# Layer B's Strassen operand sums: by adding DMA from DRAM in place of vector operations on GpSimd

## The chip, the cores and the metric

The kernel runs on one core of a Trainium2 chip. The metric is the device time of one execution in microseconds (us); smaller is better. The program works on TensorE (PE: matmuls), VectorE (DVE), ScalarE (ACT), GpSimd (POOL) and the queues from which DMA transfers are issued (SyncE, SP; ScalarE and GpSimd issue some too).

## The reference

Two layers of a decoder trunk on 1024 tokens of width 1024, in float32. Layer A is a gated MLP, layer B a Mamba-2 (SSD) mixer; each adds its output to the residual, and a last RMSNorm follows. What concerns the change is layer B's input projection:

```
proj   = rmsnorm(h) @ w_in                    # 1024 x 1024  times  1024 x 6176
z      = proj[..., :2048]                     # gate, silu(z) multiplies the output
xbc    = silu(conv(proj[..., 2048:6144]))     # causal convolution of 4 taps along the tokens
dt     = softplus(proj[..., 6144:] + dt_bias) # 32 heads; decays exp(cumsum(dt * A)) come from it
```

## The kernel before, in words

**Products.** float32 matmuls are made of three in the fast format: an operand is split into a high part (a rounding cast on ScalarE, `split`, L111) and a low part (the difference, L112, on VectorE), and `mm3` (L134 to L136) adds high x high, low x high and high x low into one accumulator. In tile names `wh` and `wl` are a weight operand's two parts, `hh` and `hl` those of the activations.

**Blocks.** Most of layer B's input projection is done in eight `Block`s. A block multiplies the 1024 tokens by 512 columns of w_in (256 in the half block) as a 2 x 2 product with seven half-size products in place of eight (Strassen's scheme in Winograd's form). The weight quarters are b00, b01 (upper half of the rows, left and right columns) and b10, b11. Four sums of them are needed:

```
t1 = b01 - b00        (L204, operand of product 5)
t2 = b11 - t1         (L205, operand of product 6)
t7 = b11 - b01        (L214, over b01, operand of product 7)
t4 = b10 - t2         (L212, over b10, operand of product 4)
```

Products 1, 2 and 3 take b00, b10 and b11 as they are. `Block.prep(n)` makes an operand (with its sum, when it has one) and splits it; `Block.mm(n, i)` issues the matmuls of unit i; `Block.post` hands a finished quarter to the block's `done`; `Block.run` does all in the order 1, 2, 6, 7, 4, 5, 3. Each quarter is loaded by SyncE (`load_raw`, L120). The sums run on the block's engine `eng`.

**Which blocks, in order.** Block 0 to 3 give z (`z_block`, block 3 with 128 columns in place of 256 per half), and four blocks give x and B, C of the groups 0, 1 and then 3, 5 (`xbc_block`). They run as z block 0, 1, 2; x(0,1); bc(0,1); x(3,5); z block 3; bc(3,5). Sums are on GpSimd in block 0 (the fourth on VectorE), on VectorE in z blocks 1 and 2, and on GpSimd in all the rest; z block 3 also has its low parts made on GpSimd.

**Around them.** Block 0 is interleaved by hand with the end of layer A (`into_b`, a manual schedule): the residual rows are normalised (`norm`, L971), transposed on TensorE (L977), and GpSimd forms sums of activations (`s31`, L1014 and L1015) and the start of each row's 1/sqrt (`rsqrt_a`, tile `rr`, L141). Behind product 6 of z block 1 stand the `decays` (L1140 to L1189): a chain of small VectorE operations from `dtr` to dt (L1146 to L1158), scans, three pairs of transposes on TensorE (L1186), and SyncE's writes of `cs_d`, `ecs_d` and of `dec_d`, whose elements are single numbers. Everywhere but in `into_b` a scheduler orders the instructions of each engine by its own estimates; each engine then works through its list strictly in order, and an instruction that waits holds up all behind it.

**What leaves a block.** A z quarter goes through a tile `zt` (pool k2, three buffers; sum on VectorE L913, silu on ScalarE L915) and is written to DRAM by GpSimd's queue (`z_d`, L917). An xbc quarter is added on VectorE into `u` (L1240), and `convolve` works off the convolution's taps (VectorE, L1205, and L1208 for the few columns at the seam, `halo`), with ScalarE before and after. `u` also names the tile to which ScalarE copies a product (L252). Raw weights have four buffers (`wr`), high and low parts three each, accumulators six.

Of the kernel before, what the change touches and what calls it, by code (L numbers as in the profile page):

```python
# [11 lines left out]
ALU = mybir.AluOpType  # L12
# [3 lines left out]
P = 128  # L16
# [13 lines left out]
def kernel(  # L30
# [21 lines left out]
    nc = tc.nc  # L52
    x = x[0]
    out = out[0]
# [13 lines left out]
    def q4(shape, name):  # L68
        return sb.tile(shape, F32, name=name, tag="q4", bufs=6)
# [112 lines left out]
    class Block:  # L182
# [5 lines left out]
        def __init__(self, H, W, token_major, done, eng=nc.vector, cols=256):  # L188
            self.H, self.W, self.token_major, self.done, self.eng = H, W, token_major, done, eng
            self.cols, self.units = cols, 2 if token_major else cols // P  # L190
            self.b, self.Y, self.acc, self.u, self.wide, self.t2 = {}, {}, {}, {}, False, None

        def load(self, kh, j):
            self.b[kh, j] = load_raw(self.W(kh, j), 4)

        def sums(self):
            if self.t2 is None:
                b, TT = self.b, self.eng.tensor_tensor
                if self.wide:
                    t12 = s8([P, 2, 4, 256], "t12")  # L200
                    self.t1, self.t2 = t12[:, 0], t12[:, 1]
                else:
                    self.t1, self.t2 = q4([P, 4, self.cols], "t1"), q4([P, 4, self.cols], "t2")
                TT(out=self.t1, in0=b[0, 1], in1=b[0, 0], op=ALU.subtract)  # L204
                TT(out=self.t2, in0=b[1, 1], in1=self.t1, op=ALU.subtract)  # L205

        def prep(self, n, lo=None):
            b, TT = self.b, self.eng.tensor_tensor
            if n in (4, 6):
                self.sums()  # L210
            if n == 4:
                TT(out=b[1, 0], in0=b[1, 0], in1=self.t2, op=ALU.subtract)  # L212
            if n == 7:
                TT(out=b[0, 1], in0=b[1, 1], in1=b[0, 1], op=ALU.subtract)  # L214
            src = {1: b[0, 0], 2: b[1, 0], 4: b[1, 0], 7: b[0, 1], 3: b[1, 1]}.get(n)
            if src is None:
                src = self.t1 if n == 5 else self.t2
            h_, l_ = wh([P, 4, self.cols]), wl([P, 4, self.cols])
            split(h_, l_, src, lo)
            self.Y[n] = (h_, l_)  # L220

        def mm(self, n, i, post=True, halves=(0, 1)):
            Xh, Xl = self.H[("A11", "A12", "S4", "A22", "S1", "S2", "S3")[n - 1]]
# [340 lines left out]
    for g in range(G):  # L564
# [26 lines left out]
        def mix(m, th):  # L591
            c = g * 2 + m
            mx = sm("mx")
            for q in range(4):
# [11 lines left out]
        blk = Block(HS, lambda kh, j: [a_w_in[kh * 512:(kh + 1) * 512, j * DI + g * 256:j * DI + (g + 1) * 256]],  # L606
                    False, done_zu)
# [10 lines left out]
    class Out:  # L618
# [82 lines left out]
        def add(self, dst, src):  # L701
            nc.gpsimd.dma_start(out=dst, in_=src, accum_op=ALU.add)
# [154 lines left out]
    H2 = {}  # L857
# [47 lines left out]
    def z_block(b, eng=nc.vector):  # L905

        wide = 256 if b < 3 else 128

        def done(name, i, a, u):
            th, j = 2 - int(name[1]), int(name[2]) - 1  # L910
            zt = k2([P, 512], "zt")
            if u is not None:
                nc.vector.tensor_tensor(out=zt, in0=a, in1=u, op=ALU.add)  # L913
                a = zt
            nc.scalar.activation(zt, a, AF.Silu)  # L915
            g, m = (2 * b + j, i) if b < 3 else (6, j)
            nc.gpsimd.dma_start(out=z_d[g][:, m, th * 512:(th + 1) * 512], in_=zt)  # L917

        def W(kh, j):
            c = 512 * b + j * wide  # L920
            return [b_w_in[kh * 512:(kh + 1) * 512, c:c + wide]]

        return Block(H2, W, False, done, eng, wide)

    def dt_load():

# [30 lines left out]
    zb = [z_block(b) for b in range(4)]  # L957

    def into_b():


        V, S, Gp = nc.vector, nc.scalar, nc.gpsimd
        TTv, TTg = V.tensor_tensor, Gp.tensor_tensor
        blk = zb[0]
# [52 lines left out]
        def s2(tt):  # L1017
            f0 = F[1, tt][:, 0]
            TTv(out=f0, in0=F[0, tt][:, 1], in1=f0, op=ALU.subtract)
            hi("S2", tt, f0)  # L1020
            lo("S2", tt, f0)
# [49 lines left out]
        ao.post(3, 3), ao.rstd_a(0, 3), store_h1(0, 3, 1)  # L1071
        second(1)
        s31(1)
        blk.sums()
        norm(0, 3, rs(3))
        s2(0), both("S3", 0, S3[0])
        blk.prep(2)
# [2 lines left out]
        second(2)  # L1080
        s31(2)
        s2(1), both("S3", 1, S3[1])
        blk.mm(1, 0, False)
        tr(0, 3)
        second(3)
        s31(3)
        blk.eng = V
        blk.prep(4)
        blk.eng = Gp
        s2(2), s2(3)  # L1090
        blk.mm(1, 1, False)
        for i in range(2):
# [38 lines left out]
        for i in range(2):  # L1131
            blk.post(3, i), nxt.post(1, i)

    zb[0].eng, zb[0].wide = nc.gpsimd, True
    with tc.manual_schedule():
        into_b()
    tok_of = {}
    V = nc.vector
# [75 lines left out]
    def xbc_block(kind, gs):  # L1214

        held, halos = {}, {}

        def cols(j):
            if kind == "x":
                return [(DI + gs[j] * 256, 256)]  # L1220
            return [(2 * DI + j * 1024 + g * P, P) for g in gs]

        def W(kh, j):
            return [b_w_in[kh * 512:(kh + 1) * 512, c:c + n] for c, n in cols(j)]

        def out(th, i, j, src, halo=None):
            if kind == "x":
                g, m, c = gs[j], i, cols(j)[0][0] + i * P
            else:
                g, m, c = gs[i], 2 + j, cols(j)[i][0]  # L1230
            dst = k2([P, 512], "xc")
            for op in conv_ops(dst, src, (c - DI) // P, halo):
                op()
            nc.scalar.activation(dst, dst, AF.Silu)
            nc.scalar.dma_start(out=xbc_d[g][:, th, m, :], in_=dst)

        def done(name, i, a, u):
            th, j = 2 - int(name[1]), int(name[2]) - 1
            if u is not None:
                nc.vector.tensor_tensor(out=u, in0=a, in1=u, op=ALU.add)  # L1240
# [12 lines left out]
        b = Block(H2, W, False, done, nc.gpsimd)  # L1253
        b.wide = True
        return b

# [560 lines left out]
```

## Time and profile before

| | |
|---|---|
| median of 3 runs | 1625.0 us (1624.87 to 1628.37) |
| the profiled execution | 1622.94 us |
| its span, first to last instruction | 1621.2 us |
| mean granted TensorE clock | 0.969 |
| GpSimd busy | 466.8 us (29%) |
| VectorE busy | 1085.5 us (67%) |

The profile has one row per instruction with its start from the span's beginning, its duration, the engine, the line of the kernel, the tiles (output <- inputs, `x` and a number for equal instructions drawn together), and in brackets how long the engine had stood idle before it and what ended that. The waits view adds these idle times up by pair: who waited, for whom, total, times, longest. A DMA row gives the transfer's size and the median time from issue to landing. z block 0 begins at about 720 us and bc(3,5) ends at about 1070 us.

### The profile page before, as it was taken

The page shows a single profiled execution, that of the slowest core. Times are in us where ns is not written, and L with a number is a line of the kernel's source. Part 1 is how long each engine was busy: PE and PEld are TensorE (multiplying, and loading weights), DVE is VectorE, ACT ScalarE, POOL GpSimd, SP SyncE. Part 2 cuts the span into 40 slices and gives each one's busy share as a digit, 9 for nine tenths or more (in the row PEclk, how much of TensorE's full clock was granted, in tenths as well). Part 3 has the DMA queues.
Part 4 walks back from the last instruction along what each step waited for, and adds up shares of the span by engine and source line. Part 5 has one row for each costly group of instructions (what it writes and reads, how often), then busy time and mean ns, then how long its engine had stood idle before and what let it go on. Part 6 is the DMA issues. An engine that isn't in the chain of part 4 may idle for free. (4 is left out here: it accounts for less than half of the span.)

```text
span 1621.2 us, 21245 instructions
## 1 busy us (share of the span) xinstructions
PE 1514.6 (93%) x7832; PEld 1246.8 (77%) x7832; DVE 1085.5 (67%) x1669; ACT 757.0 (47%) x1239; POOL 466.8 (29%) x477
## 2 busy tenths in 40 slices
PE   5899999999999999997899998999999999889988
PEld 4799988888888878775678776777777767657776
DVE  6966566666666545577743788587777777657646
ACT  4522232333223345554543454456666576544454
POOL 3601110000000131234203223316766766221231
PEclk9899999999999999998999999999999999979999
DMA  5153333233334999932253222547666665795993
GB/s 171 44 185 135 106 98 109 101 104 109 109 109 167 297 263 238 191 104 65 83 108 113 83 98 85 175 134 206 172 173 183 171 188 143 228 239 179 223 241 113
DMA packets 164872, 244.89 MB, mean 151 GB/s; under 512 B 16048, under 2 KB 96800, under 8 KB 161568
## 3 DMA queue, kind: packets, MB, share of 16 engines
q1 hardware_dynamic: 134672, 166.43, 34.1%
q0 software_dynamic: 20928, 63.45, 17.2%
q10 hardware_dynamic: 9168, 13.64, 2.3%
q8 instruction: 62, 1.02, 0.3%
q14 instruction: 42, 0.34, 0.1%
HBM read 169.23 MB, written 51.18 MB: 136 GB/s over the span
## 5 line engine op out<-in xcount | busy, mean ns | idle before, releaser
L134 PE MATMUL acc<-hh,wh 128*128 128x512 f32 x868 | 345.3, 398 | 14.5 <-ACT wh L111 4.2
L135 PE MATMUL acc<-hl,wh 128*128 128x512 f32 x868 | 342.8, 395 | 4.4 <-DVE hl L989 4.4
L136 PE MATMUL acc<-hh,wl 128*128 128x512 f32 x868 | 342.5, 395 | 3.8 <-DVE wl L112 3.0
L112 DVE TENSOR_TENSOR wl<-wr,wh 128x1024 fp32r<-128x1024 f32 x94 | 122.9, 1310 | 128.8 <-ACT wh L111 128.8
L134 PEld LDWEIGHTS acc<-hh,wh 128*128 128x128 f32 x868 | 165.8, 191 | 52.0 <-DVE u L1240 5.2
L136 PEld LDWEIGHTS acc<-hh,wl 128*128 128x128 f32 x868 | 165.8, 191 | 41.3 <-DVE wl L112 4.8
L135 PEld LDWEIGHTS acc<-hl,wh 128*128 128x128 f32 x868 | 165.9, 191 | 38.7 <-DVE hl L989 4.8
L111 ACT CAST wh<-wr 128x1024 fp32r<-128x1024 f32 (+1 forms) x113 | 116.2, 1030 | 115.8 <-PE acc L135 78.7
L252 ACT COPY u<-acc 128x512 f32<-128x512 f32 x117 | 68.0, 582 | 187.2 <-PE acc L136 185.9
L136 PE MATMUL acc<-wh,hl 128*128 128x256 f32 x448 | 131.3, 293 | 11.5 <-DVE hl L355 11.5
L134 PE MATMUL acc<-wh,hh 128*128 128x256 f32 x448 | 132.1, 295 | 4.2 <-DVE vt L291 2.5
L135 PE MATMUL acc<-wl,hh 128*128 128x256 f32 x448 | 130.7, 292 | 1.1 <-DVE wl L365 1.1
L1424 ACT ACTIVATE wl<-wl,tk 128x128 f32<-128x128 f32 x256 | 82.1, 391 | 88.2 <-DMA wl<-cs_d 87.7
L134 PE MATMUL ab<-hh,wh 128*128 128x512 f32 x256 | 115.5, 451 | 2.2 <-DVE u L1240 2.2
L136 PE MATMUL ab<-hh,wl 128*128 128x512 f32 x256 | 100.8, 394 | 0.0
L135 PE MATMUL ab<-hl,wh 128*128 128x512 f32 x256 | 100.1, 391 | 0.0
L136 PEld LDWEIGHTS acc<-wh,hl 128*128 128x128 f32 x448 | 89.9, 201 | 12.5 <-DVE hl L355 12.5
L134 PE MATMUL bo<-wh,xh 128*128 128x512 f32 x192 | 80.9, 421 | 14.6 <-ACT wh L111 5.7
L134 PEld LDWEIGHTS acc<-wh,hh 128*128 128x128 f32 x448 | 90.0, 201 | 5.2 <-issue 2.9
L112 DVE TENSOR_TENSOR xl<-ya,xh 128x1024 fp32r<-128x1024 f32 x40 | 49.1, 1228 | 64.3 <-ACT xh L111 64.2
L135 PEld LDWEIGHTS acc<-wl,hh 128*128 128x128 f32 x448 | 90.0, 201 | 1.6 <-DVE wl L365 1.4
L605 POOL DMA_DIRECT2D y_d<-y x8 | 4.4, 548 | 291.8 <-DVE y L602 291.8
(316 smaller groups left out, 3379.6 us busy)
## 6 DMA issues: line engine op xcount, KB each, us to landing
wr<-in_a_w_in_dram SPq DMA_DIRECT2D x48, 512.0 KB, 3.6
wl<-cs_d SPq DMA_DIRECT2D x64, 256.0 KB, 3.6
wr<-in_b_w_in_dram SPq DMA_DIRECT2D x30, 512.0 KB, 4.8
ya<-ya POOLq DMA_DIRECT2D x28, 512.0 KB, 14.7
wb<-in_a_w_out_dram SPq DMA_DIRECT2D x10, 1024.0 KB
wb<-in_b_w_out_dram SPq DMA_DIRECT2D x10, 1024.0 KB, 18.2
wr<-in_b_w_in_dram SPq DMA_DIRECT2D x36, 256.0 KB, 4.4
v<-v_d SPq DMA_DIRECT2D x8, 1024.0 KB, 4.9
```

The costliest lines, as they stand in the source:

```text
L111: nc.scalar.copy(out=hi, in_=src)
L112: return (eng or nc.vector).tensor_tensor(out=lo, in0=src, in1=hi.bitcast(F32), op=ALU.subtract)
L134: nc.tensor.matmul(out=o, lhsT=l[0], rhs=r[0], start=start, stop=False, **kw)
L135: nc.tensor.matmul(out=o, lhsT=l[0], rhs=r[1], start=False, stop=False, **kw)
L136: nc.tensor.matmul(out=o, lhsT=l[1], rhs=r[0], start=False, stop=stop, **kw)
L252: nc.scalar.copy(out=self.u[n][:, i], in_=a)
L605: store = lambda: nc.gpsimd.dma_start(out=y_d[-1], in_=y)
L1424: nc.scalar.activation(wl[:, j, :], wl[:, j, :], AF.Relu, scale=-1.0, bias=tokc(2, c, self.g)[:, j:j + 1])
```

## The change

In every block of layer B the four sums are made by transfers that add to what their destination in on-chip memory holds. The weights are read a second time from DRAM for it. The signs are made by ScalarE:

```
t2 = -b01             then  t2 += b00,  t2 += b11      (two transfers, the second behind the first)
t7: b01 = -b01        then  b01 += b11
t1 = -b00             then  t1 += b01
t4: b10 = -t2         then  b10 += b10 from DRAM
```

The first three are begun right behind the split of operand 1, the fourth behind that of operand 6. Each block so has four ScalarE passes and five transfers of 512 KB (a bc block ten of 256 KB, since its columns lie in two places; z block 3 five of 256 KB). GpSimd issues them. z block 3's low parts are made on VectorE.

```diff
+        def add(self, dst, kh, j):
+            o = 0
+            for w in self.W(kh, j):
+                n = w.shape[1]
+                nc.gpsimd.dma_start(out=dst[:, :, o:o + n], in_=w.rearrange("(k p) n -> p k n", p=P),
+                                    accum_op=ALU.add)
+                o += n
+
+        def sums_by_transfer(self):
+            b, neg = self.b, lambda o, i: nc.scalar.mul(o, i, -1.0)
+            neg(self.t2, b[0, 1])
+            self.add(self.t2, 0, 0)
+            neg(b[0, 1], b[0, 1])
+            self.add(b[0, 1], 1, 1)
+            neg(self.t1, b[0, 0])
+            self.add(self.t2, 1, 1)
+            self.add(self.t1, 0, 1)
...
         def prep(self, n, lo=None):
...
             if n == 4:
-                TT(out=b[1, 0], in0=b[1, 0], in1=self.t2, op=ALU.subtract)
-            if n == 7:
-                TT(out=b[0, 1], in0=b[1, 1], in1=b[0, 1], op=ALU.subtract)
+                self.fourth()
+            elif n == 7 and self.eng:
+                self.eng.tensor_tensor(out=b[0, 1], in0=b[1, 1], in1=b[0, 1], op=ALU.subtract)
...
             self.Y[n] = (h_, l_)
+            if self.eng is None:
+                if n == 1:
+                    self.sums()
+                elif n == 6:
+                    self.fourth()
+
+        def fourth(self):
+            b = self.b[1, 0]
+            if self.t4:
+                return
+            self.t4 = True
+            if self.eng is None:
+                nc.scalar.mul(b, self.t2, -1.0)
+                self.add(b, 1, 0)
+            else:
+                self.eng.tensor_tensor(out=b, in0=b, in1=self.t2, op=ALU.subtract)
...
-        return Block(H2, W, False, done, eng, wide)
+        return Block(H2, W, False, done, None, wide)
...
-        blk.sums()
         norm(0, 3, rs(3))
...
         s2(1), both("S3", 1, S3[1])
+        blk.fourth()
         blk.mm(1, 0, False)
...
-        blk.eng = V
         blk.prep(4)
-        blk.eng = Gp
...
-        b = Block(H2, W, False, done, nc.gpsimd)
+        b = Block(H2, W, False, done, None)
...
-            zb[3].eng = nc.gpsimd
-            zb[3].run(unit=convolve, lo=nc.gpsimd)
+            zb[3].run(unit=convolve)
```

What moves on the engines is shown at three places. Line numbers of the changed kernel run up to 40 higher. First GpSimd in `into_b`, from the activation sums of row 0 to the first z writes; `rr` is row 3's 1/sqrt, the four pairs of `s` and `nrm` are the rows 0 to 3. Before:

```order
L1014 TENSOR_TENSOR s_5727<-f,nrm 128x512
L1015 TENSOR_TENSOR nrm<-nrm 128x512
L141 TENSOR_TENSOR rr<-stats,mhalf 128x1
L1014 TENSOR_TENSOR s_5787<-f,nrm 128x512
L1015 TENSOR_TENSOR nrm<-nrm 128x512
L204 TENSOR_TENSOR t_5790<-wr 128x1024
L205 TENSOR_TENSOR t_5790<-wr,t_5790 128x1024
L1014 TENSOR_TENSOR s_5841<-f,nrm 128x512
L1015 TENSOR_TENSOR nrm<-nrm 128x512
L1014 TENSOR_TENSOR s_5878<-f,nrm 128x512
L1015 TENSOR_TENSOR nrm<-nrm 128x512
L214 TENSOR_TENSOR wr<-wr 128x1024
```

And in the changed kernel (L202 is the adding transfer):

```order
L1054 TENSOR_TENSOR s_5727<-f,nrm 128x512
L1055 TENSOR_TENSOR nrm<-nrm 128x512
L202 DMA t_5734<-in_b_w_in_dram 128x4x256
L202 DMA wr<-in_b_w_in_dram 128x4x256
L202 DMA t_5734<-in_b_w_in_dram 128x4x256 x2
L141 TENSOR_TENSOR rr<-stats,mhalf 128x1
L1054 TENSOR_TENSOR s_5795<-f,nrm 128x512
L1055 TENSOR_TENSOR nrm<-nrm 128x512
L1054 TENSOR_TENSOR s_5846<-f,nrm 128x512
L1055 TENSOR_TENSOR nrm<-nrm 128x512
L202 DMA wr<-in_b_w_in_dram 128x4x256
L1054 TENSOR_TENSOR s_5885<-f,nrm 128x512
```

Four adds now stand ahead of `rr`, the third of them behind the landing of the first; the three sums are gone.

Second the decays in z block 1, on VectorE: from the operand of the dt chain's first row to dtr. Before, with the block's last two sums and the lows of products 7, 4 and 5 in between (`t_6246` is t2, `t_6245` t1):

```order
L214 TENSOR_TENSOR wr<-wr 128x1024
L1152 TENSOR_SCALAR dtw<-dtw 128x256
L212 TENSOR_TENSOR wr<-wr,t_6246 128x1024
L913 TENSOR_TENSOR zt<-acc,u 128x512
L1154 SCALAR_TENSOR_TENSOR dtw<-dtw 128x256
L112 TENSOR_TENSOR wl<-wr,wh 128x1024
L1154 SCALAR_TENSOR_TENSOR dtw<-dtw 128x256
L112 TENSOR_TENSOR wl<-wr,wh 128x1024
L1154 SCALAR_TENSOR_TENSOR dtw<-dtw 128x256 x4
L112 TENSOR_TENSOR wl<-t_6245,wh 128x1024
```

And in the changed kernel:

```order
L112 TENSOR_TENSOR wl<-wr,wh 128x1024
L1190 TENSOR_SCALAR dtw<-dtw 128x256
L1192 SCALAR_TENSOR_TENSOR dtw<-dtw 128x256
L953 TENSOR_TENSOR zt<-acc,u 128x512
L1192 SCALAR_TENSOR_TENSOR dtw<-dtw 128x256
L112 TENSOR_TENSOR wl<-wr,wh 128x1024
L1192 SCALAR_TENSOR_TENSOR dtw<-dtw 128x256 x5
L1193 SCALAR_TENSOR_TENSOR dtw<-dtw 128x256
L1194 TENSOR_SCALAR dtw<-dtr 128x256
L1196 SCALAR_TENSOR_TENSOR dtr<-dtw 128x256
```

The sums are gone, and the two lows that stay in front of the chain's end read operands that a transfer completes. On TensorE the two transposes of dtr move 15 matmuls ahead, to right behind the first matmul of a unit of product 7 (order of TensorE before, then changed, around them):

```order
L134 MATMUL acc<-hh,wh 128x512
L135 MATMUL acc<-hl,wh 128x512
L136 MATMUL acc<-hh,wl 128x512
L134 MATMUL acc<-hh,wh 128x512
L1186 MATMUL tp<-ident,dtr 128x128 x2
L135 MATMUL acc<-hl,wh 128x512
```

```order
L135 MATMUL acc<-hl,wh 128x512
L136 MATMUL acc<-hh,wl 128x512
L134 MATMUL acc<-hh,wh 128x512
L1224 MATMUL tp<-ident,dtr 128x128 x2
L135 MATMUL acc<-hl,wh 128x512
L136 MATMUL acc<-hh,wl 128x512
```

Only their place moved; the matmuls around them are the same.

Third GpSimd from z block 1 to x(0,1). Before, only the z writes of the blocks (`z_d` and a number for the group):

```order
L917 DMA z_d_5290<-zt 128x512 x2
L917 DMA z_d_5291<-zt 128x512 x2
L917 DMA z_d_5292<-zt 128x512 x4
L917 DMA z_d_5293<-zt 128x512 x4
L917 DMA z_d_5294<-zt 128x512 x2
```

And in the changed kernel (`t_6500`, `t_6499` are z block 2's t2 and t1, `t_6761` is that of x(0,1)):

```order
L957 DMA z_d_5292<-zt 128x512 x2
L202 DMA t_6500<-in_b_w_in_dram 128x4x256
L202 DMA t_6499<-in_b_w_in_dram 128x4x256
L202 DMA wr<-in_b_w_in_dram 128x4x256
L202 DMA t_6500<-in_b_w_in_dram 128x4x256
L957 DMA z_d_5292<-zt 128x512 x2
L957 DMA z_d_5293<-zt 128x512
L202 DMA t_6761<-in_b_w_in_dram 128x4x256
L957 DMA z_d_5293<-zt 128x512 x2
```

Four adds of z block 2 stand between z block 1's writes, and the fourth adds to what the first has filled.

More of the change, by code (lines that the diff above doesn't have):

```diff
@@ L191, in __init__ @@
             self.b, self.Y, self.acc, self.u, self.wide, self.t2 = {}, {}, {}, {}, False, None
+            self.t4 = False
         def load(self, kh, j):
             self.b[kh, j] = load_raw(self.W(kh, j), 4)
+        def add(self, dst, kh, j):
[14 more added lines that the diff above has]
+            self.add(self.t1, 0, 1)
         def sums(self):
             if self.t2 is None:
-                b, TT = self.b, self.eng.tensor_tensor
+                b = self.b
                 if self.wide:
@@ L203, in sums @@
                     self.t1, self.t2 = q4([P, 4, self.cols], "t1"), q4([P, 4, self.cols], "t2")
+                if self.eng is None:
+                    return self.sums_by_transfer()
+                TT = self.eng.tensor_tensor
                 TT(out=self.t1, in0=b[0, 1], in1=b[0, 0], op=ALU.subtract)
@@ L207, in prep @@
         def prep(self, n, lo=None):
-            b, TT = self.b, self.eng.tensor_tensor
+            b = self.b
             if n in (4, 6):
@@ L220, in prep @@
             self.Y[n] = (h_, l_)
+            if self.eng is None:
[8 more added lines that the diff above has]
+            self.t4 = True
+            if self.eng is None:
+                nc.scalar.mul(b, self.t2, -1.0)
+                self.add(b, 1, 0)
+            else:
+                self.eng.tensor_tensor(out=b, in0=b, in1=self.t2, op=ALU.subtract)
         def mm(self, n, i, post=True, halves=(0, 1)):
@@ L903, with z_block @@
     z_d = [dr.tile([P, 2, T], F32, name=f"z_d{g}") for g in range(G)]
-    def z_block(b, eng=nc.vector):
+    def z_block(b):
         wide = 256 if b < 3 else 128
@@ L1132, in into_b @@
             blk.post(3, i), nxt.post(1, i)
-    zb[0].eng, zb[0].wide = nc.gpsimd, True
+    zb[0].wide = True
     with tc.manual_schedule():
```

## Prediction

> **What bounds the kernel now.** I read the page first, then the waits of TensorE over layer B's input projection (720 to 1070 us, where all edited blocks run), then the timelines around its stalls. From the page, and from the waits (engine, line, released by: total us, times, longest):
>
> ```profile
> span 1621.2 us, 21245 instructions
> PE 1514.6 (93%) x7832; PEld 1246.8 (77%) x7832; DVE 1085.5 (67%) x1669; ACT 757.0 (47%) x1239; POOL 466.8 (29%) x477
> L111 ACT CAST wh<-wr 128x1024 fp32r<-128x1024 f32 (+1 forms) x113 | 116.2, 1030 | 115.8 <-PE acc L135 78.7
> wr<-in_b_w_in_dram SPq DMA_DIRECT2D x30, 512.0 KB, 4.8
> ```
>
> ```profile
> PE tp L977 <- DVE nrm L971: 5.4, 2, 3.3
> PE acc L135 <- DVE hl L989: 4.4, 1, 4.4
> PE acc L134 <- ACT wh L111: 4.2, 2, 2.8
> PE acc L134 <- DVE u L1240: 4.0, 3, 2.9
> PE acc L134 <- DVE zt L913: 3.6, 1, 3.6
> ```
>
> TensorE is the bound at 93%; the 107 us without a matmul are all that any edit can win, and these rows hold 22 of them. The edit does not shorten a matmul, so only such rows can change, and the clock that follows a stall. One of them shows how GpSimd matters although TensorE never waits for it here (start us, us; TensorE's idle time in brackets):
>
> ```profile
> 905.16 2.97 DVE L1205 SCALAR_TENSOR_TENSOR xc<-u,par,xc 128x510 f32<-128x510 f32 x1
> 908.04 2.33 DVE L1208 SCALAR_TENSOR_TENSOR xc<-halo,par,xc 128x2 f32<-128x2 f32 x1
> 910.30 0.74 DVE L1205 SCALAR_TENSOR_TENSOR xc<-u,par,xc 128x509 f32<-128x509 f32 x1
> ```
>
> ```profile
> 905.18 2.39 POOL L205 TENSOR_TENSOR t<-wr,t 128x1024 f32<-128x1024 f32 x1 [7.25 <-DMA wr<-in_b_w_in_dram]
> 907.53 2.83 POOL L214 TENSOR_TENSOR wr<-wr 128x1024 f32<-128x1024 f32 x1
> ```
>
> ```profile
> 912.48 0.80 PE L134 MATMUL acc<-hh,wh 128*128 128x512 f32 x1 [2.89 <-DVE u L1240]
> 913.08 0.63 PE L135 MATMUL acc<-hl,wh 128*128 128x512 f32 x1
> 913.50 0.63 PE L136 MATMUL acc<-hh,wl 128*128 128x512 f32 x1
> ...
> 916.24 0.39 PE L134 MATMUL acc<-hh,wh 128*128 128x512 f32 x1
> 916.46 0.39 PE L135 MATMUL acc<-hl,wh 128*128 128x512 f32 x1
> ```
>
> A convolution tap takes 0.74 us, 2.97 beside GpSimd's sum; even the tap on 2 columns takes 2.33. `u` is late by that, TensorE stands 2.89 us and then runs slow: matmuls are 0.42 us apart (913.08 to 913.50) instead of 0.22. From 912.48 to 916.24 lie nine steps, 3.76 us instead of some 2.05 at full speed: 1.7 us on top. So a stall of about 3 us costs 4.6. The Trainium skill ("TensorE: Matmul & The Clock Gate", "What's actually happening") has the clock fall after an idle window of about 3.4 us. By that page a stall of 2.89 us would cost nothing more; this row says otherwise and decides.
>
> **What the change prices at, apiece.** An added negation is a ScalarE pass over 128x1024: the cast of that size takes 1.03 us (row above), three per block at the start and one more for the fourth sum. An added sum is a GpSimd-issued transfer of 512 KB. Nearest rows, an adding transfer's landing in layer A (from 440 to 640 us) and the issue time of the same line:
>
> ```profile
> ya<-y_d POOLq DMA_DIRECT2D x4, 512.0 KB, 6.9
> ```
>
> ```profile
> L702 POOL DMA_DIRECT2D ya<-y_d x4: 1058/1082/1116, 532.9 to 562.0; - x4
> ```
>
> Between a plain load (4.8) and the adding transfer in heavier traffic (6.9) I take 5.8 us to land and 1.1 to issue. The second addend into t2 must wait for the first, so t2 is ready about 1.0 + 5.8 + 5.8 = 12.6 us after b01 has loaded, where the two sums on GpSimd took 2.39 us each. The Trainium skill ("DMA: Bandwidth & Descriptors", "Anatomy of one DMA") gives 2.0 us plus bytes at 436 GB/s. By that page an add would land in about 3.2 us (an estimate) and the chain would take 7.4; no row of this trace that adds 512 KB from memory shows it.
>
> **Stage 1, the entry into layer B (block 0).** Norm of row 3, then the product on the fourth sum:
>
> ```profile
> 727.94 0.54 POOL L141 TENSOR_TENSOR rr<-stats,mhalf 128x1 f32<-128x1 f32 x1 [4.67 <-DVE stats L845]
> 731.68 2.34 POOL L204 TENSOR_TENSOR t<-wr 128x1024 f32<-128x1024 f32 x1
> ```
>
> ```profile
> 721.28 1.06 ACT L111 CAST wh<-wr 128x1024 fp32r<-128x1024 f32 x1 [0.66 <-ACT nrm L1008]
> 731.77 5.54 DVE L971 SCALAR_TENSOR_TENSOR nrm<-u,stats,nwb 128x512 f32<-128x512 f32 x2
> 737.24 0.68 DVE L1019 TENSOR_TENSOR f<-nrm,f 128x512 f32<-128x512 f32 x1
> 749.66 3.40 DVE L112 TENSOR_TENSOR wl<-wr,wh 128x1024 fp32r<-128x1024 f32 x1 [1.11 <-ACT wh L111]
> ```
>
> The norm's two halves took 5.54 us where two operations of that size take some 1.4 (0.68 apiece in the next row): 4.1 us lost beside L204 and the sum behind it, and TensorE waited 5.4 for it. But now GpSimd's row-3 `rr` stands behind the adds. The first negation ends at 722.3 + 1.0, the second add into t2 waits until about 723.4 + 5.8 = 729.2, two issues follow, and `rr` starts near 731.4 instead of 727.94: 3.4 us later. Net gain 0.7. At the fourth sum `wl` falls from 3.40 to 1.2 us, but the sum itself must now land; between nothing and 2.2 gained. I take -1.5 for the stage; ends -3.5 (`rr` not held up) and +1 (adds at 6.9).
>
> **Stage 2, block 1 with the decays.** VectorE loses four sums of 1.22 us here, yet the decays are not freed: their chain on VectorE now has the lows of products 7 and 4 in front of its last eight rows, and these wait for transfers. TensorE's transposes of dtr moved up 15 matmuls. Block 1's first cast, a sum that goes, the end of the decays' chain, and TensorE:
>
> ```profile
> 786.75 1.04 ACT L111 CAST wh<-wr 128x1024 fp32r<-128x1024 f32 x1
> 803.68 1.22 DVE L214 TENSOR_TENSOR wr<-wr 128x1024 f32<-128x1024 f32 x1
> 814.08 0.42 DVE L1158 SCALAR_TENSOR_TENSOR dtr<-dtw 128x256 f32<-128x256 f32 x1
> ```
>
> ```profile
> 810.70 0.39 PE L134 MATMUL acc<-hh,wh 128*128 128x512 f32 x1
> ...
> 814.55 0.44 PE L1186 MATMUL tp<-ident,dtr 128*128 128x128 f32 x2
> ```
>
> TensorE now asks for dtr behind the matmul of 810.70, so at 810.9. Block 1's first negation follows its first cast and ends at 788.8; the first addend of t2 lands at 794.6, the second at 800.4. ScalarE casts t2 (801.4) and, after a z activation, negates it for the fourth (some 803); that add lands near 809, its cast and low take it to 811, and behind these stand six decay operations of 0.42 us and two smaller: dtr at about 814, 3.5 us too late, and 7 where each of the three adds takes 6.9. Matmuls after such a stall run slow (1.7). I take +5.5; ends +2 (three adds at 4.8) and +9.
>
> **Stage 3, block 1 into block 2.** Here the memory queues are already jammed by the decays' own tiny transfers, and a z tile is not free until its write has landed:
>
> ```profile
> DMA to landing us min/median/max: 8.0/9.5/11.0
> ```
>
> ```profile
> 821.61 0.54 POOL L917 DMA_DIRECT2D z_d<-zt  x1 [12.87 <-ACT zt L915]
> 833.79 0.69 DVE L913 TENSOR_TENSOR zt<-acc,u 128x512 f32<-128x512 f32 x1 [7.56 <-DMA z_d<-zt]
> 834.54 0.80 PE L134 MATMUL acc<-hh,wh 128*128 128x512 f32 x1 [3.60 <-DVE zt L913]
> ```
>
> (The first row is of dec_d, from issue to landing.) In the new order four adds of block 2 are issued ahead of block 1's last z writes, and the fourth waits for the first. If that add, issued near 820, takes the 9.5 to 12 us of its neighbours, GpSimd is held until 830 to 832, the write behind it lands at 834 to 842, and TensorE's 3.6 us stall grows by 0 to 8. I take +2, since only one of the remaining writes stands behind the waiting add.
>
> **Stage 4, the three full convolution blocks.** GpSimd has no tensor work left there, the adds have a dozen us of slack (a product is 24 matmuls of 0.23, 5.5 us; t2 is used at the third), so the 912 stall goes with its clock, -4.6, and two of the smaller stalls on `u` (4.0 - 2.9 = 1.1), -0.9: -5.5, ends -5.7 and +2 (a late t2).
>
> **Stage 5, half block 3 and the block behind it.**
>
> ```profile
> 1006.20 0.50 PE L134 MATMUL acc<-hh,wh 128*128 128x512 f32 x1 [2.83 <-ACT wh L111]
> 1007.68 0.50 PE L136 MATMUL acc<-hh,wl 128*128 128x512 f32 x1 [0.75 <-POOL wl L112]
> 1013.40 0.50 PE L134 MATMUL acc<-hh,wh 128*128 128x512 f32 x1 [1.57 <-ACT u L252]
> 1019.29 0.50 PE L134 MATMUL acc<-hh,wh 128*128 128x512 f32 x1 [1.17 <-ACT u L252]
> ```
>
> 6.3 us of stalls, and after the first, as at 912, some 1.7 of slow clock. All come from VectorE and ScalarE running behind GpSimd's sums, and the lows move from GpSimd to VectorE. What is late next: the t2 of the block behind needs two times two adds of 256 KB, with z writes in between, and its third product comes 11 us after its first. I take -5; ends -8 and +2. Past 1070 us nothing is edited, and all that shifts.
>
> **The sum.** -1.5 + 5.5 + 2 - 5.5 - 5 = -4.5 us against the profiled execution of 1622.9 us (span 1621.2 and 1.7 around it). That run lies 2.1 under the median of 1625.0, so the forecast is 1625.0 - 4.5 = 1620.5 us.
>
> **Rivals.** (a) The GpSimd queue becomes the bound, slower. One mechanism: an add that waits for its predecessor holds z writes and later adds, zt tiles run out, TensorE stalls at blocks 1 to 3. Stages 2 and 3 at their ends (+9, +8), 4 and 5 halved (-2.8, -2.5), stage 1 as above: +10, 1635 us. It decides where block 1's z write, issued at 821.61 before, lands after about 838. For it: VectorE's 7.56 us wait for just such a write. Against it: adds and z writes elsewhere have free queues. Chance 0.25. (b) Wash: stages 4 and 5 win only their stalls' first half, since ScalarE's four negations of 1.03 us stand ahead of the same `u` copies: -1.5 + 5.5 + 2 - 2.8 - 2.5, within 1 us of before, 1625. Chance 0.25. (c) Quick adds: each lands like a plain load or sooner. Then stage 2 is at +2, stage 3 at 0, the others at their good ends but stage 1 at -2: 2 - 2 - 5.7 - 8 = -13.7, 1611 us. Chance 0.12. The price that the Trainium skill gives for an add ("DMA: Bandwidth & Descriptors", "Anatomy of one DMA") points here. That GpSimd keeps its sums can be ruled out from the order. My forecast has 0.38.
>
> **How the numbers follow.** A measurement can tell about 0.2%, 3.2 us. Faster holds (c) and most of the forecast, 0.12 + 0.36 = 0.48; same the wash and the rest, 0.25; slower (a) and a little, 0.27. For 8 in 10 the range runs from (c), 1611, to (a), 1635. The forecast's own range is 1616 to 1624.
>
> **What would show it.** Right: no DVE tap over 1.5 us from 900 to 1000; no stall on `u` near 912; a new stall of 2 to 5 us on the transposes of dtr (L1224); the zt stall near 834 no shorter than 3.6; `rr` of row 3 about 3 us later. Wrong: adds landing in under 4 us, or dtr in time (then (c)); z writes held by more than 15 us, or a t2 cast of any block that TensorE waits for (then (a)).

## The result and the profile after

The changed kernel takes 1672.0 us (median of 4 runs, 1663.9 to 1674.2), the kernel before beside it 1626.7 (4 runs). The ratio is 1.0269, with a 95% interval from 1.0229 to 1.0309: some 44 us slower, where 4.5 us faster were forecast. Executions of the kernel before scatter from 1618 to 1632 us over all chips used, so everything below goes by ratios to the kernel before on the same chip. The changed kernel's profiled execution took 1663.9 us.

From the page of the changed kernel: the span, the engines, and GpSimd's transfer queue with its packets, MB and share of the 16 transfer engines' time.

```profile
span 1662.2 us, 21338 instructions
PE 1517.4 (91%) x7832; PEld 1248.2 (75%) x7832; DVE 1044.8 (63%) x1667; ACT 785.6 (47%) x1271; POOL 467.7 (28%) x497
q0 software_dynamic: 47328, 83.12, 25.5%
```

The same row of the kernel before:

```profile
q0 software_dynamic: 20928, 63.45, 17.2%
```

VectorE lost 41 us of work, and TensorE's work is the same. What grew is the queue's share: 25.5% of 1662 us less 17.2% of 1621 us is 145 us of all 16 engines, for 19.7 MB. By this estimate (the difference holds also what the other packets of the queue gained or lost) an add of 512 KB occupies all 16 transfer engines for 3.9 us. TensorE's waits in the changed kernel from 720 to 1110 us:

```profile
PE acc L134 <- ACT u L292: 21.1, 7, 8.6
PE acc L134 <- DVE zt L953: 18.3, 1, 18.3
PE tp L1017 <- DVE nrm L1011: 5.4, 1, 5.4
PE acc L134 <- ACT wh L111: 5.2, 1, 5.2
...
PE tp L1224 <- DVE dtr L1196: 3.1, 1, 3.1
```

The wait for `u` behind VectorE's taps (L1240, 4.0 us before) is gone, as forecast. In its place stand 21.1 us for ScalarE's copies `u` and 18.3 us for one `zt`. Where the time went can be read from the start of the same matmul (the k-th of 7832) in both traces:

| stage, to matmul | before, us | after, us | behind | in this stage | forecast |
|---|---|---|---|---|---|
| ahead of block 0, 3648 | 705.59 | 703.43 | -2.2 | | |
| 1, entry, 4008 | 805.71 | 806.25 | +0.5 | +2.7 | -1.5 |
| 2, decays, 4056 | 816.68 | 824.76 | +8.1 | +7.5 | +5.5 |
| 3, into z block 2, 4128 | 837.80 | 861.29 | +23.5 | +15.4 | +2 |
| 4, three full convolution blocks, 4724 | 979.64 | 1001.95 | +22.3 | -1.2 | -5.5 |
| 5, z block 3 and bc(3,5), 5064 | 1068.83 | 1108.43 | +39.6 | +17.3 | -5 |
| the rest, 7800 | 1605.82 | 1646.74 | +40.9 | +1.3 | 0 |

**Stage 3** holds the longest stall. GpSimd's issues there, then VectorE and TensorE, then two stretches with (after engines' busy times) the clock, the transfer engines' share and GB/s:

```profile
825.49 2.67 POOL L202 DMA_DIRECT2D t<-in_b_w_in_dram  x2 [10.67 <-ACT t L207]
828.81 1.26 POOL L202 DMA_DIRECT2D wr<-in_b_w_in_dram  x1 [0.66 <-DVE wl L112]
840.94 1.28 POOL L202 DMA_DIRECT2D t<-in_b_w_in_dram  x1 [10.87 <-DMA t<-in_b_w_in_dram]
841.69 2.21 POOL L957 DMA_DIRECT2D z_d<-zt  x3
```

```profile
834.04 0.69 DVE L953 TENSOR_TENSOR zt<-acc,u 128x512 f32<-128x512 f32 x1 [0.63 <-PE acc L136]
856.97 0.69 DVE L953 TENSOR_TENSOR zt<-acc,u 128x512 f32<-128x512 f32 x1 [22.23 <-DMA z_d<-zt]
```

```profile
857.71 0.80 PE L134 MATMUL acc<-hh,wh 128*128 128x512 f32 x1 [18.27 <-DVE zt L953]
```

```profile
825.00:840.00 15.00, 14.45 (x64) 11.64 (x62) 3.14 (x3) 8.62 (x11) 3.93 (x3) 1.00 0.71 52
840.00:858.00 18.00, 0.29 (x1) 0.29 (x2) 1.03 (x2) 1.32 (x2) 3.12 (x5) 0.56 1.04 186
```

The second addend of t2 waits 10.87 us in GpSimd's list for the first. Three z writes stand behind it, go out together at 841.7 and land at 856.9 to 858.1; three of the four adds have not landed when they go out. Until then VectorE has no `zt` and TensorE does one matmul in 18 us. In the first stretch the transfer engines are 71% occupied and move only 52 GB/s. Almost all of that time (10.1 of 10.7 us) stands in the trace under adding packets, of which some last up to 7 us; the packets of single numbers have 0.1 us. It is the decays' writes that make them so long: from 815 to 862 us the longest adding packet takes 7.0 us here, and 0.9 and 1.1 us in the two programs further below that have adds but no `dec_d`. In the second stretch the engines are full.

**Stage 5** has the other form. ScalarE in z block 3 and bc(3,5):

```profile
1029.83 0.62 ACT L111 CAST wh<-wr 128x512 fp32r<-128x512 f32 x1 [5.13 <-DMA wr<-in_b_w_in_dram]
1035.68 0.81 ACT L1249 ACTIVATE xc<-u,par 128x512 f32<-128x512 f32 x1 [3.15 <-DMA xbc_d<-xc]
1036.40 0.56 ACT L292 COPY u<-acc 128x512 f32<-128x512 f32 x1
...
1073.63 1.04 ACT L111 CAST wh<-wr 128x1024 fp32r<-128x1024 f32 x1 [8.68 <-DMA wr<-in_b_w_in_dram]
```

```profile
1037.01 0.80 PE L134 MATMUL acc<-hh,wh 128*128 128x512 f32 x1 [8.61 <-ACT u L292]
1075.22 0.79 PE L134 MATMUL acc<-hh,wh 128*128 128x512 f32 x1 [5.23 <-ACT u L292]
```

ScalarE waits in its list for t4's add (5.13, 8.68 us) and for a convolution tile `xc`, which is free only when its write to xbc_d has landed (3.15). The copies of products stand behind these waits, and TensorE behind the copies. For the whole kernel, the adds' landing (min, median, max, from the view of L202), then who waited for an xbc write and those writes' landing:

```profile
DMA to landing us min/median/max: 4.6/7.7/23.4
```

```profile
DMA xbc_d<-xc: 19.0, 11
...
DMA to landing us min/median/max: 2.0/3.6/5.6
```

Before, these writes landed in 2.0 us in the median, and ScalarE waited 2.4 us for them in all:

```profile
ACT xc L1211: 2.4, 4
...
DMA to landing us min/median/max: 2.0/2.0/3.9
```

### The profile page after: what moved, and what is told of

Read it like the earlier page. It is cut to its first block, busy times and chain, and to the rows that moved or that the text cites. A ratio compares the mean times of both kernels' runs of the same rounds, so it can differ in the third digit from the quotient of the medians.

```text
span 1662.2 us, 21338 instructions
## 1 busy us (share of the span) xinstructions
PE 1517.4 (91%) x7832; PEld 1248.2 (75%) x7832; DVE 1044.8 (63%) x1667; ACT 785.6 (47%) x1271; POOL 467.7 (28%) x497
## 3 DMA queue, kind: packets, MB, share of 16 engines
q0 software_dynamic: 47328, 83.12, 25.5%
## 4 chain that ended last, share of the span: by engine, by line
PE 42%; issue 19%; DMA 18%; DVE 8%; ACT 7%; POOL 4%; SPq 1%; ACTq 0%; POOLq 0%; DVEq 0%
PE acc L136 8%; PE acc L134 8%; PE acc L135 8%; DMA wl<-cs_d 4%; PE ab L134 2%; DMA ya<-ya 2%; PE ab L136 2%; PE ab L135 2%; DMA wb<-in_b_w_out_dram 2%; DMA xbc_d<-xc 2%; DMA wr<-in_b_w_in_dram 2%; PE yy L1487 1%; DMA t<-in_b_w_in_dram 1%; PE yy L1491 1%; DVE wl L112 1%
## 5 line engine op out<-in xcount | busy, mean ns | idle before, releaser
L134 PEld LDWEIGHTS acc<-hh,wh 128*128 128x128 f32 x868 | 167.2, 193 | 84.3 <-ACT u L292 25.5
L112 DVE TENSOR_TENSOR wl<-wr,wh 128x1024 fp32r<-128x1024 f32 (+1 forms) x99 | 118.6, 1199 | 156.0 <-ACT wh L111 155.8
L136 PEld LDWEIGHTS acc<-wh,hl 128*128 128x128 f32 x448 | 90.3, 202 | 14.6 <-DVE hl L395 14.6
```

The costliest lines, as they stand in the source:

```text
L112: return (eng or nc.vector).tensor_tensor(out=lo, in0=src, in1=hi.bitcast(F32), op=ALU.subtract)
L134: nc.tensor.matmul(out=o, lhsT=l[0], rhs=r[0], start=start, stop=False, **kw)
L136: nc.tensor.matmul(out=o, lhsT=l[1], rhs=r[0], start=False, stop=stop, **kw)
```

## The experiments

The theory after the result has two parts: **load** (adding transfers occupy the transfer engines so long that writes of z and xbc, whose landing frees a tile, queue behind them) and **lists** (GpSimd and ScalarE, working strictly in order, hold other work behind an add that has not landed). The first four runs only ask for the place.

**Which blocks.** Edit: per block, `eng` is None or the engine before.

```diff
-    zb = [z_block(b) for b in range(4)]
+    zb = [z_block(b, e) for b, e in enumerate((None, nc.vector, nc.vector, None))]   # all but z 1, 2
```

> Adding transfers in every block but z blocks 1 and 2, whose four sums go back to VectorE. Theory of places (late landings cost where an in-order list waits for them: the trace has +7 us at the dtr transposes and +16 at block 1's last z writes, +17 in z block 3 and bc(3,5), -4 at the 912 us stall): 1627 + 45 - 24 = 1648 us, no stall over 4 us between 800 and 860. Rival theory of load (each of 36 whole adds loads the transfer engines and costs 1.25 us wherever it is): 10 adds fewer, 1672 - 12.5 = 1659 us.

> Adding transfers in z blocks 1 and 2 alone, all other blocks as before. Theory of places: 1627 + 24 = 1651 us, with the zt stall near 857 us at 15 us or more. Rival theory of load: 10 adds, 1627 + 12.5 = 1639 us.

> Adding transfers in x(0,1), bc(0,1) and x(3,5) alone. Theory of places: only the stall at 912 us goes, and a small one on wl at the end of z block 2 is absent: 1627 - 4 = 1623 us. Rival theory of load: 15 whole adds, 1627 + 19 = 1646 us.

> Adding transfers in z block 3 (lows on VectorE) and bc(3,5) alone. Theory of places: 1627 + 15 = 1642 us, with the stalls on ScalarE's u copies (8.6, 5.2 us in the changed kernel) in place of the four of 6.3 us before. Rival theory of load: 7.5 whole adds, 1627 + 9 = 1636 us.

| adds in | ratio | 95% interval | us |
|---|---|---|---|
| all but z blocks 1, 2 | 1.0083 | 1.0055 to 1.0112 | +14 |
| z blocks 1, 2 alone | 1.0136 | 1.0101 to 1.0170 | +22 |
| x(0,1), bc(0,1), x(3,5) alone | 1.0044 | 1.0026 to 1.0063 | +7 |
| z block 3, bc(3,5) alone | 1.0079 | 1.0051 to 1.0107 | +13 |

The two large places are those of the trace: 22 of 24 us expected in z 1 and 2, 13 of 15 in the tail; proportion to the number of adds would give 12 and 9. The run without z 1 and 2 came out below both expectations, 14 us where 21 and 32 stood, so the places don't simply add up. And the convolution blocks, for which -4 was expected, are not faster. In that run's waits from 720 to 1110 us:

```profile
PE acc L136 <- DVE wl L112: 5.6, 3, 2.7
...
PE acc L134 <- DVE zt L953: 4.7, 2, 3.2
```

The wait on taps is gone, and a low part is late instead (5.6 us; 3.0 before). There ScalarE waited 3.4 and 3.3 us for xbc writes ahead of its casts. A part of the +7 lies past 1070 us, where nothing is edited: at matmul 5064 that profile was 4.5 us behind, at 7800 10.0.

**Load or order.** The same program with plain loads in place of the adds, so the sums are left out. Every engine's order stays word for word.

```diff
-                                    accum_op=ALU.add)
+                                    )
```

> The changed kernel with its 50 added transfers as plain loads (nothing is added, so the sums are left out and the output is wrong); order and waits of every engine stay word for word the same. Theory of load (an adding packet of 1 KB occupies a transfer engine 101 ns where a plain one takes 46 to 60, and z and xbc writes queue behind them): the stall on zt near 857 us falls from 18 to under 9 us, those near 1037 and 1075 by half, 1645 us or less. Rival theory of waits (the new order alone holds GpSimd's and ScalarE's lists, whatever a transfer takes): over 1660 us.

Ratio 1.0053 (1.0035 to 1.0071): some 9 us are left of 44. From that kernel's waits, from the view of its transfers (issue time in ns; landing), and from its page:

```profile
PE acc L134 <- DVE zt L952: 12.3, 1, 12.3
PE acc L134 <- ACT u L291: 7.7, 4, 3.4
```

```profile
L202 POOL DMA_DIRECT2D t<-in_b_w_in_dram x30: 747/748/846, 724.5 to 1025.6; - x30
...
DMA to landing us min/median/max: 3.4/4.7/17.4
```

```profile
q0 software_dynamic: 26528, 83.12, 21.7%
```

The load theory holds for the sum, and the wait for `u` copies falls to a third. But the stall on zt only falls to 12.3 us (under 9 was expected). With the same order, four fifths of the loss come with the adding: landing 7.7 against 4.7 us, GpSimd's issue 1.3 us in the changed kernel against 0.75, and by the queue's share 74 us of all transfer engines (21.7% of 1627 us less 17.2% of 1621 us) against 145. The edit changes more than the arithmetic, though. The same 83.12 MB go in 26528 packets in place of 47328: the adds move in packets of 1 KB and 512 bytes, the plain loads in packets of 4 KB. What the adding costs and what the small packets cost, this run does not part.

The 9 us are also a net figure. In the table by stages further below, plain loads still cost 14.6 us in stages 2 and 3 and gain 12.0 in stages 1 and 4.

> z blocks 1 and 2 alone with added transfers, but as plain loads (sums left out, output wrong); same order and waits as with adding ones, which gave a ratio of 1.0136, +22 us. Theory of load: less than half of that is left, a ratio of 1.006 or less, the zt stall under 13 us. Rival theory of order and waits: 1.011 or more.

In z blocks 1 and 2 alone plain loads leave 1.0097 (1.0067 to 1.0128) of 1.0136: between the two expectations, and the intervals overlap. In this place order and waits seem to carry most; the two ratios are too near each other to show it.

**GpSimd's list.** The changed kernel with its z writes issued by ScalarE.

```diff
-            nc.gpsimd.dma_start(out=z_d[g][:, m, th * 512:(th + 1) * 512], in_=zt)
+            nc.scalar.dma_start(out=z_d[g][:, m, th * 512:(th + 1) * 512], in_=zt)
```

> The changed kernel with the z writes issued by ScalarE, which has just made them, in place of GpSimd. Theory of load (the adds occupy the transfer engines; who issues the z writes does not matter): the stall on zt near 857 us stays over 12 us, 1660 us or more. Rival theory of GpSimd's list (z writes come late because they stand behind an add that waits): that stall falls to about 4 us and the time by 15 us or more, 1655 us or less.

Ratio 1.0136 (1.0105 to 1.0167), half of the loss gone. The stall of 18.3 us is now two:

```profile
837.21 0.77 PE L134 MATMUL acc<-hh,wh 128*128 128x512 f32 x1 [4.94 <-DVE zt L953]
...
846.23 0.79 PE L134 MATMUL acc<-hh,wh 128*128 128x512 f32 x1 [4.03 <-DVE zt L953]
```

The list theory wins this one against load alone, with two reservations. A write that ScalarE issues also goes through another queue than the adds: counted from matmul 4056, the write that frees the tile goes out 4.4 us earlier than in the changed kernel and takes 3.0 us less to land (12.2 instead of 15.2). And the scheduler orders the engines anew in this program, so not all that differs is the list. Plain loads save 35 us and ScalarE's writes 22, more than 44 together, so the two overlap. We read it so: an add that lands late holds the list, and the list holds writes that then queue beside more adds.

**The decays' tiny writes.** The eight `dec_d` transfers left out, in three programs.

```diff
-                nc.sync.dma_start(out=dec_d[2 * q + j].rearrange("(h o) -> h o", o=1),
-                                  in_=ecs[rs_, j * P + P - 1:j * P + P])
...
-        nc.sync.dma_start(out=decb, in_=dec_d.rearrange("c h -> (c h)").partition_broadcast(P))
+        nc.sync.dma_start(out=decb, in_=cs_d[0, 0:2].rearrange("h l -> (h l)").partition_broadcast(P))
```

> Adding transfers in z blocks 1 and 2 alone (1645 us), and the decays' eight writes of single numbers to dec_d left out (the chunk decays are read from cs_d in their place, so the output is wrong). Theory that dec_d's tiny writes and the adds jam together: the 16.8 us stall on zt falls to under 5 us, 1628 us. Rival theory that four adds ahead of the z writes do it alone: the stall stays over 12 us, 1640 us or more.

> The changed kernel with the z writes issued by ScalarE and without dec_d's eight writes (chunk decays read from cs_d in their place, output wrong). Theory that block 1's last z writes were late from two causes, GpSimd's list and dec_d's jam: both stalls on zt (4.9 and 4.0 us with ScalarE's writes alone) fall below 2 us, and 1644.5 becomes 1634 us. Rival theory that the adds alone fill the transfer engines there: they stay over 3 us each, 1641 us or more.

> The kernel before without dec_d's eight writes (output wrong), the control for the two runs without them. If dec_d costs the same with and without adds: the 3.6 us stall on zt near 834 us goes, 5 us off, a ratio of 0.997; the adds' interplay with it then is the rest, some 5 us of the 10 seen. If dec_d matters only beside adds: 1.000.

With adds in z 1 and 2: 1.0076 (1.0047 to 1.0106) in place of 1.0136, the stall on zt 5.3 in place of 16.8 us; the time is half-way between the two expectations. With ScalarE's z writes: 1.0063 (1.0039 to 1.0086) in place of 1.0136, no stall on zt. In the kernel before: 0.9965 (0.9946 to 0.9984). So some 6 us of it are dec_d's own price, which the kernel before pays too. The 4 to 6 us that are left for its meeting with the adds lie within the intervals of these ratios. Stage 3 of the traces shows the meeting more clearly: without dec_d that stage is 11.5 us shorter with adds in z 1 and 2 and 13.2 with ScalarE's writes, but only 5.2 in the kernel before. By stages, from the same matmuls as in the table of the result (one profiled execution each):

| stage | changed | plain loads | z writes by ScalarE | the same, no dec_d |
|---|---|---|---|---|
| 1 | +2.7 | -5.8 | -2.7 | -3.1 |
| 2 | +7.5 | +5.2 | +5.8 | +5.8 |
| 3 | +15.4 | +9.4 | +8.0 | -5.2 |
| 4 | -1.2 | -6.2 | +0.3 | -2.4 |
| 5 | +17.3 | +0.2 | +9.4 | +10.7 |

Stage 3 is list, load and dec_d together. With list and dec_d away nothing of the loss remains: the kernel before without dec_d is 5.2 us shorter there too. Stage 5 needs the slow adds: with plain loads it is nil. Stage 2 costs 5 us or more whatever is done. In all four programs ScalarE stands there at the cast of t2 until its second add has landed, but what TensorE then waits for differs: dtr (3.1 us) in the first two, a low part (2.1 us) with ScalarE's z writes, where the order is another.

**Is there a gain to be had from freeing GpSimd?** The sums on VectorE, without a transfer:

```diff
-        b = Block(H2, W, False, done, nc.gpsimd)
+        b = Block(H2, W, False, done, nc.vector)     # first run: not in bc(3,5)
...
-            zb[3].eng = nc.gpsimd
-            zb[3].run(unit=convolve, lo=nc.gpsimd)
+            zb[3].run(unit=convolve)                 # second run only
```

> No adding transfer anywhere; the sums of x(0,1), bc(0,1) and x(3,5) move from GpSimd to VectorE (12 sums of 1.2 us). Theory that only GpSimd's sums beside VectorE's taps made the 912 us stall, and that VectorE has the room: 1627 - 4.6 = 1622 us, no tap over 1.5 us from 900 to 1000. Rival theory that VectorE, busy 60% of that time, becomes late itself: other stalls on u or wl of 3 us or more, 1627 us or above.

> As the run with VectorE's sums in the three full convolution blocks, and also those of z block 3 (with its low parts) and of bc(3,5) on VectorE. Theory of GpSimd beside VectorE: the four stalls of 6.3 us from 1006 to 1019 us and their slow clock go too, 1627 - 4.6 - 8 = 1614 us. Rival theory that VectorE is then late in z block 3, whose products last 2.7 us: 1625 us or above.

0.9996 (0.9977 to 1.0014) and 0.9993 (0.9977 to 1.0009): neither moves the time by what can be told. TensorE's waits from 860 to 1000 us in the first of them:

```profile
PE acc L136 <- DVE wl L112: 3.3, 2, 1.7
PE acc L134 <- ACT wh L111: 2.8, 1, 2.8
```

The kernel before in the same stretch of time:

```profile
PE acc L134 <- DVE u L1240: 4.0, 3, 2.9
```

The 912 us stall is gone (no tap over 0.75 us there), and two waits of 1.65 us on low parts are new (the 2.8 of ScalarE is z block 3's, which begins 7 us earlier in this run). In this trace stage 4 is 2.8 us shorter where 5.5 were sought. So even without the price of the adds, about half of that gain is taken back on the next engine.

**Half the transfers.** Only t1 and t7 by one add each, t2 and t4 on VectorE.

```diff
+            nc.scalar.mul(self.t1, b[0, 0], -1.0)
+            self.add(self.t1, 0, 1)
+            nc.scalar.mul(b[0, 1], b[0, 1], -1.0)
+            self.add(b[0, 1], 1, 1)
```

> z block 3 and bc(3,5): only t1 and t7 by one adding transfer each (no chain of two), t2 and t4 by VectorE, lows on VectorE; every other block as before. All four sums by transfer in these two blocks gave +13 us (ratio 1.0079). Theory of load with many writers (the xbc writes wait for the adds, half the adds, half the delay): 1.003, +5 us. Rival theory that the chain to t2 and the late t4 did it: 1.000, the stalls on u copies near 1012 and 1050 us gone.

> x(0,1), bc(0,1), x(3,5): only t1 and t7 by one adding transfer each, t2 and t4 by VectorE; every other block as before. All four by transfer gave +7 us (ratio 1.0044), all four on VectorE 0 (0.9996). Theory of load: the xbc writes land in 3 us instead of 4.2, a ratio of 1.001 to 1.003. Rival theory of the t2 chain: as on VectorE, 0.998 to 1.000.

> t1 and t7 by one adding transfer each, t2 and t4 on VectorE, in x(0,1), bc(0,1), x(3,5), z block 3 and bc(3,5); z blocks 0 to 2 as before. If the two runs with half the transfers (0.9984 and 0.9986) add up: 0.997, some 5 us faster than before. Rival: their gains are the measurement's spread, 0.999 to 1.001.

0.9984 (0.9966 to 1.0003), 0.9986 (0.9968 to 1.0004), and both together 0.9999 (0.9984 to 1.0014). The price is gone with the chain and half the load, but no gain is shown; the first two don't add up. The load theory expected 1.003 in the tail and 1.001 to 1.003 in the convolution blocks, and both intervals end below that. So the slow adds don't seem to cost a fixed price each, but through what waits for t2's second add and for the late t4. The edit takes away the chain and half the adds at once, so this is argued and not shown.

**A version that beats both.** The chunk decays spread on the chip, in the kernel before with its sums where they were:

```diff
+        for j in range(2):
+            V.tensor_scalar(dg[:, j * P:(j + 1) * P], ident, ecs[:, j * P + P - 1:j * P + P], None, ALU.mult)
+        nc.tensor.matmul(out=tp[:, 0:256], lhsT=ones, rhs=dg, start=True, stop=True)
+        nc.scalar.copy(out=decb.rearrange("p (q j h) -> p j q h", q=4, j=2),
+                       in_=tp[:, 0:256].rearrange("p (j q h) -> p j q h", j=2, q=4))
-                nc.sync.dma_start(out=dec_d[2 * q + j].rearrange("(h o) -> h o", o=1),
-                                  in_=ecs[rs_, j * P + P - 1:j * P + P])
-        nc.sync.dma_start(out=decb, in_=dec_d.rearrange("c h -> (c h)").partition_broadcast(P))
```

> The kernel before, with the chunk decays brought to all partitions on the chip (two diagonal products on VectorE, one matmul with ones of 128x256, one ScalarE copy) in place of eight writes of single numbers and a broadcast read. If the 3.6 us stall on zt near 834 us and its slow clock come from the writes to dec_d: a ratio of 0.9965 as with the writes left out, less some 1 us for the matmul: 0.997, 1618 us. Rival theory that z writes and loads collide there anyway: 0.999 to 1.000.

0.9965 (0.9951 to 0.9979), 1619.0 us against 1625.3. The landing of the z writes in this kernel, then in the kernel before:

```profile
DMA to landing us min/median/max: 2.3/2.6/4.6
```

```profile
DMA to landing us min/median/max: 2.3/3.3/12.1
```

The stall on zt is gone from 780 to 900 us, where the kernel before has it:

```profile
PE acc L134 <- DVE zt L913: 3.6, 1, 3.6
```

## Why the prediction was wrong

The step that failed is "What the change prices at, apiece": an add was priced as its own landing of 5.8 us, and at nothing for the transfers beside it. 5.8 us was about the quickest of the 25 adds of 512 KB (5.9); the median was 7.7, and the longest took 23.4. The adds' place on the transfer engines slowed the others as well (xbc writes 2.0 to 3.6 us in the median, z writes 3.3 to 5.0), and that half has no term in the sum at all. Plain loads in the same order, which land sooner and take half the engines' time, leave 9 us of the 44. They do not tell which of the two halves weighs more.

Stage 1: the mechanism was right on one side. `rr` came 3.7 us later, counted from matmul 3648 (3.4 was forecast), and the norm then ran unhindered, as these rows of GpSimd and VectorE show:

```profile
727.95 2.57 POOL L202 DMA_DIRECT2D t<-in_b_w_in_dram  x2 [3.66 <-DMA t<-in_b_w_in_dram]
729.47 1.63 POOL L141 TENSOR_TENSOR rr<-stats,mhalf 128x1 f32<-128x1 f32 x1
```

```profile
733.98 1.41 DVE L1011 SCALAR_TENSOR_TENSOR nrm<-u,stats,nwb 128x512 f32<-128x512 f32 x2
```

Norm 1.41 us instead of 5.54, but TensorE waited 5.4 us for it as before, and 5.2 for the fourth sum, on whose landing ScalarE's cast hung:

```profile
750.49 1.04 ACT L111 CAST wh<-wr 128x1024 fp32r<-128x1024 f32 x1 [5.30 <-DMA wr<-in_b_w_in_dram]
```

-1.5 was forecast and +2.7 came, outside the ends of -3.5 and +1: the fourth sum, put at "between nothing and 2.2 gained", cost its landing.

Stage 2 was right in place and near in size (+5.5 forecast, +7.5 measured), but not in its cause. dtr was ready too late for transposes that had moved up, a 3.1 us stall. Two waits on u copies ahead of it make another 2.8 us, and a third of 1.8 stands just ahead of the stage.

```profile
817.60 0.43 DVE L1196 SCALAR_TENSOR_TENSOR dtr<-dtw 128x256 f32<-128x256 f32 x1
```

```profile
818.08 0.57 PE L1224 MATMUL tp<-ident,dtr 128*128 128x128 f32 x2 [3.07 <-DVE dtr L1196]
```

The prediction had the lows of products 7 and 4 wait for their adds in VectorE's list. They ran without a wait. ScalarE was what held the chain: the function that opens it (L1185, L1147 before) had moved behind the cast of t2, and that cast waited for the second add. In the changed kernel, then in the kernel before:

```profile
802.49 1.05 ACT L111 CAST wh<-t 128x1024 fp32r<-128x1024 f32 x1 [8.39 <-DMA t<-in_b_w_in_dram]
...
806.94 0.42 ACT L1185 ACTIVATE dtw<-dtw 128x256 f32<-128x256 f32 x1
```

```profile
796.78 0.42 ACT L1147 ACTIVATE dtw<-dtw 128x256 f32<-128x256 f32 x1
...
799.74 1.03 ACT L111 CAST wh<-t 128x1024 fp32r<-128x1024 f32 x1
```

Nor did the stall on dtr follow the landing, as the ends of +2 and +9 assumed: with plain loads that cast waited 3.9 us instead of 8.4, and the stall was 3.1 us again. So the nearness of +5.5 is partly luck.

Stage 3 had the right mechanism as rival (a), and the wrong choice. "I take +2, since only one of the remaining writes stands behind the waiting add": three stood there, and they went out together. Rival (a)'s point of decision, a landing after 838, was passed by 19 us. But its top, +8, took a write's landing among the decays' writes alone; with the adds in the same queue the stage lost 15.4 us. Moving the writes to ScalarE's queue halved it, and taking dec_d away as well ended it.

Stage 4: the stall at 912 us went, as priced (-4.6), and every tap there took 0.75 us. What is late next was put at nothing. ScalarE, held by xbc writes, gave the taps and then a low part late, and 2.3 us of stall came back at 947 us:

```profile
944.08 2.07 DVE L1243 SCALAR_TENSOR_TENSOR xc<-u,par,xc 128x511 f32<-128x511 f32 x3 [2.39 <-ACT xc L1249]
946.07 1.22 DVE L112 TENSOR_TENSOR wl<-wr,wh 128x1024 fp32r<-128x1024 f32 x1
```

With plain loads this stage gained 6.2 us (forecast 5.5), so here the price of the adds made the difference.

Stage 5 was wrong in sign: -5 forecast, +17.3 measured, +0.2 with plain loads. The prediction looked at t2 of bc(3,5) only. t4, asked for two products after t2 and issued behind bc(3,5)'s adds, and the xbc writes were not priced. So rival (a) was too cheap as well: it left stages 4 and 5 with half their gains, and 1635 was the range's end.

Rival (c), quick adds, was refuted: the quickest add of 512 KB took 5.9 us. By the fit of the Trainium skill ("DMA: Bandwidth & Descriptors", "Anatomy of one DMA") a transfer of 512 KB that GpSimd issues takes 3.2 us (an estimate). This case's trace does not agree: even the plain loads of that size on GpSimd's queue took 4.2 us at best and 5.3 in the median.

Left open: how much of the 35 us between adds and plain loads is the adding, how much the smaller packets and how much GpSimd's longer issue, since the one edit changes all three. That half the transfers seemed to gain 0.15% in each of two places and nothing in both together lies within the scatter; a gain that small was not settled.

## What to carry to other kernels

Price a transfer by the time it takes from all others on the transfer engines, not only by its own landing, and ask first which of the others frees a buffer that an engine is waiting for. A transfer that must wait for another one does not belong in a list ahead of writes that free tiles. And a busy stretch with few GB/s (here 52 at a share of 0.71) is a reason to look for a few tiny transfers: taking eight writes of single numbers away gave 0.35%, more than any edit of the sums.

## What the runs showed of the hardware

An adding packet of 1 KB took 102 ns on its transfer engine in the median and one of 512 bytes 65 (changed kernel, 720 to 1110 us). Plain packets of these sizes on SyncE's queue took 46 and 27 ns. In the run with plain loads GpSimd's queue moved the same bytes in packets of 4 KB at 168 ns. GpSimd needs 1.3 us to issue an adding transfer of 512 KB, which is 512 packets, and 0.75 for the plain one of the same shape, which is 128. Eight transfers of 32 single numbers (8.0 to 11.0 us to land) slowed what was under way with them: beside them an adding packet took up to 7.0 us (1.1 without them), and z writes took up to 12.1 us in the kernel with them and at most 4.6 in the one that makes the values on the chip.
